# A decoder step on one core: the order of the instructions comes from another timing model of the scheduler

## The chip, the core and the metric

The kernel runs on one core of a Trainium2 chip. The core has five engines that run at the same time: PE (TensorE, matrix products), DVE (VectorE), ACT (ScalarE), POOL (GpSimd) and SP (SyncE, which here only issues transfers). Each engine runs its own instructions strictly in the order in which the program holds them; between engines there are only semaphores. An instruction that waits therefore holds up all that stands behind it on its engine, ready or not. The metric is the device time of one execution in microseconds (us).

## The reference

One inference step of a trunk of four layers over 256 prompt tokens and 8 x 4 sample tokens, model width 1024, MLP width 4096, float32. Each layer has a token mixer and an MLP; the mixers are SGU, RG-LRU, S5 and again SGU.

```python
for layer in range(DEPTH):
    h = rmsnorm(x, p['norm_mix'][layer])
    out = chunk_sgu(h, ...) | rglru_block(h, ...) | s5_block(h, ...)   # by layer % 3
    x = x + out
    x = x + sqrelu_ffn(rmsnorm(x, p['norm_ffn'][layer]), p['w_ff1'][layer], p['w_ff2'][layer])
return rmsnorm(x, p['norm_f']), ...

def rmsnorm(x, g):
    return x * lax.rsqrt(jnp.mean(x * x, axis=-1, keepdims=True) + EPS) * g
def sqrelu_ffn(h, w1, w2):
    return jnp.square(jax.nn.relu(h @ w1)) @ w2
```

RG-LRU is a projection, a causal convolution of width 4, two gates (block-diagonal products and sigmoids), a linear recurrence in time, and a product with a gelu branch before `w_out`. S5 is a complex diagonal state-space layer whose matrices follow from few parameters.

## The kernel before, in words

All activations stay on chip, features on the partitions: eight tiles `x[k]` of [128, 288 tokens]. A float32 product is made of three passes in a rounded float32 format over operands split in two: `whi*xh`, `whi*xl`, `wlo*xh` (`mm3`, lines 273 to 275). The weights are 176 chunks of 1 MiB, used one after the other. SP loads chunk after chunk (`raw`, line 179), ACT rounds it to `whi` (line 202), DVE forms the rest `wlo` (line 203), in two pieces each; there are three buffers for each of the three. Most chunks are used by 48 matmuls of 288 columns. The chunks are numbered through the layers: 0 to 11 first SGU, 12 to 43 its MLP (FFN0), 44 to 55 RG-LRU, 56 to 87 its MLP (FFN1), and so on.

A norm is applied late. `norm_tile` splits the unscaled `x` into `xh` (ACT, line 284) and `xl` (DVE, line 285); `norm_square` squares each tile (ACT, line 296, two buffers `sq`) and POOL adds the squares up in `ss` (line 297). PE sums `ss` over the features with one product with ones (line 311, tile `acc<-ss,ones`), DVE makes the factor from it (lines 315, 316), and in the MLP that factor is needed only after the second product (line 411). In the MLP, ACT takes the relu (line 388), DVE squares it (394), ACT and DVE split it into `hh` and `hl` (269, 270), and the second product uses these. The first and the second half of the MLP's width come one after the other.

The tables of the S5 layer are formed beside FFN0 and FFN1, in 49 pieces that `spare()` records between the other work. For each of eight tiles `m` of S5: `s5_inputs` (POOL) loads `bt` (line 827) and `qb` (line 830) with transfers that POOL itself issues, forms `bi` by products (836 to 838, each twice) and stores it (840); `s5_powers` and `s5_kernels` (DVE) load `cc`, `bs`, form `cn` and `bq`, PE multiplies them (line 881), POOL clears `kt` (line 884), ACT copies into it (887); `s5_table` (POOL, 897 to 906) forms `tab`. `qb`, `bt` and `bi` have two buffers, `kt` one.

The RG-LRU mixer forms its eight x tiles first (chunks 44 to 47, `evac_x`: lines 605 to 609 give the convolved `xc`), then the gates of each pair of tiles: products on PE (line 623, `sec<-xc,wab`), tanh and exp on ACT (624 to 628), the algebra on POOL and DVE (635 to 641), square root (647), the scan on DVE (660); chunks 48 to 51 form the gelu branch, POOL multiplies the two (682, 683) and splits the result into `gyh` (ACT) and `gyl` (POOL, 685), and chunks 52 to 55 are W_out.

The order in which an engine's instructions stand is not the order of the code. The library's tile scheduler orders the recorded instructions, by priorities (the place in the code; `spare()` lowers the priority of its pieces by 300 places), by dependences and buffers, and by the times at which a timing model says that an engine is free and an operand is ready:

```python
def spare(upto=0):
    if len(background) > (upto or 0):
        with tc.high_priority(offset=-PRI_SPARE):
            background.pop(0)(state['bg'])
```

## Time and profile before

| | us |
|---|---|
| median of three runs | 1320.63 (1314.42 to 1326.06) |
| span of the profiled execution | 1312.3 |
| PE, DVE, ACT, POOL busy in it | 1266.0, 926.8, 617.9, 376.4 |

The profile is one execution. A row of a timeline gives the start (us from the start of the span), the duration, the engine, the line, the operation, output and inputs with their shape, how many in a row there are, and in brackets the idle time of the engine before it and what ended it. A row of windows gives for a stretch the busy time of each engine and in brackets how many of its instructions started in it, then the clock granted to PE (1 is 2.4 GHz), the share of the transfer engines that is busy and what they moved.

### The profile page before, as it was taken

The numbers are of one execution on the slowest core, as the hardware profiler recorded it, in microseconds if no ns is written. First come the engines' busy times: TensorE is split into PE (matmuls) and PEld (weight loads), VectorE is DVE, ScalarE is ACT, GpSimd is POOL, SyncE is SP. The second block draws the span as 40 slices with busy tenths as digits, with TensorE's granted clock in tenths as the row PEclk, the third lists the DMA queues.
The fourth block names the chain that finished last, engine by engine and source line by source line (L and its number), as shares of the span: only waits on it lengthen the run. The fifth ranks groups of instructions, "written<-read, shape, count | busy, mean of one in ns | idle before, by whom it ended". The sixth has DMA issues, their size and how long they took to land.

```text
span 1312.3 us, 23910 instructions
## 1 busy us (share of the span) xinstructions
PE 1266.0 (96%) x9802; PEld 1223.4 (93%) x9802; DVE 926.8 (71%) x1437; ACT 617.9 (47%) x1019; POOL 376.4 (29%) x524
## 2 busy tenths in 40 slices
PE   8999999799979998999999999999999999999997
PEld 7999999699968997998999899999999999999997
DVE  8899759686787897748768756655666677655653
ACT  5745532354564644236443345534544645534541
POOL 2237647501258485860121200000012221000010
PEclk9999999899988998999999999999999999999998
DMA  8526666555431767546567434554446334544431
GB/s 290 207 97 205 225 185 220 181 197 194 145 121 62 232 214 243 185 153 217 182 241 257 159 131 159 177 176 162 161 161 217 135 133 160 190 161 160 161 129 37
DMA packets 47006, 230.33 MB, mean 176 GB/s; under 512 B 7904, under 2 KB 13712, under 8 KB 24368
## 3 DMA queue, kind: packets, MB, share of 16 engines
q1 hardware_dynamic: 38016, 209.63, 46.5%
q0 software_dynamic: 8016, 18.45, 4.4%
q8 instruction: 77, 1.26, 0.4%
q10 hardware_dynamic: 864, 0.72, 0.2%
q14 instruction: 33, 0.27, 0.1%
HBM read 214.17 MB, written 14.60 MB: 174 GB/s over the span
## 4 chain that ended last, share of the span: by engine, by line
PE 63%; POOL 14%; DMA 9%; DVE 8%; issue 2%; ACT 2%; SPq 0%; DVEq 0%; POOLq 0%; ACTq 0%
PE acc L275 19%; PE acc L273 19%; PE acc L274 19%; DMA qb<-qd 6%; DMA scr<-tab 3%; POOL tab L905 2%; DVE wlo L203 2%; POOL ta L903 2%; POOL tab L904 2%; POOL bi L836 2%; POOL tb L903 1%; POOL bt L837 1%; POOL bi L838 1%; PE sec L959 1%; PE sec L881 1%
## 5 line engine op out<-in xcount | busy, mean ns | idle before, releaser
L202 ACT ACTIVATE whi<-raw 128x1024 fp32r<-128x1024 f32 (+1 forms) x354 | 363.6, 1048 | 330.9 <-PE acc L274 267.0
L203 DVE TENSOR_TENSOR wlo<-raw,whi 128x1024 fp32r<-128x1024 f32 (+1 forms) x354 | 443.4, 1269 | 106.4 <-ACT whi L202 104.6
L273 PE MATMUL acc<-xh,whi 128*128 128x288 f32 x1472 | 442.3, 301 | 8.0 <-ACT whi L202 7.1
L275 PE MATMUL acc<-xh,wlo 128*128 128x288 f32 x1472 | 440.1, 300 | 7.1 <-DVE wlo L203 7.0
L274 PE MATMUL acc<-xl,whi 128*128 128x288 f32 x1472 | 434.4, 295 | 2.1 <-DVE xl L285 2.1
L273 PE MATMUL acc<-hh,whi 128*128 128x288 f32 x1024 | 305.5, 298 | 3.9 <-ACT hh L269 3.9
L274 PE MATMUL acc<-hl,whi 128*128 128x288 f32 x1024 | 304.7, 298 | 1.1 <-DVE hl L270 1.1
L275 PE MATMUL acc<-hh,wlo 128*128 128x288 f32 x1024 | 303.2, 296 | 0.0
L273 PEld LDWEIGHTS acc<-xh,whi 128*128 128x128 f32 x1472 | 278.6, 189 | 12.5 <-ACT whi L202 8.1
L275 PEld LDWEIGHTS acc<-xh,wlo 128*128 128x128 f32 x1472 | 277.7, 189 | 11.8 <-DVE wlo L203 10.1
L274 PEld LDWEIGHTS acc<-xl,whi 128*128 128x128 f32 x1472 | 282.2, 192 | 5.9 <-DVE xl L285 3.4
L297 POOL TENSOR_TENSOR ss<-ss,sq 128x288 f32<-128x288 f32 x62 | 67.7, 1092 | 566.5 <-ACT sq L296 566.0
L273 PEld LDWEIGHTS acc<-hh,whi 128*128 128x128 f32 x1024 | 192.6, 188 | 7.3 <-ACT hh L269 4.7
L274 PEld LDWEIGHTS acc<-hl,whi 128*128 128x128 f32 x1024 | 192.9, 188 | 4.5 <-issue 2.6
L275 PEld LDWEIGHTS acc<-hh,wlo 128*128 128x128 f32 x1024 | 193.6, 189 | 2.4 <-issue 2.2
L411 DVE TENSOR_TENSOR t<-acc,r 128x288 f32<-128x288 f32 x64 | 29.1, 455 | 138.8 <-PE acc L275 138.8
L269 ACT ACTIVATE hh<-t 128x288 fp32r<-128x288 f32 x128 | 56.9, 444 | 125.6 <-DVE t L394 125.6
L270 DVE TENSOR_TENSOR hl<-t,hh 128x288 fp32r<-128x288 f32 x128 | 63.3, 495 | 25.8 <-ACT hh L269 24.4
L394 DVE TENSOR_TENSOR t<-t 128x288 f32<-128x288 f32 x128 | 64.8, 506 | 4.7 <-ACT t L388 4.7
L388 ACT ACTIVATE t<-acc 128x288 f32<-128x288 f32 x128 | 51.0, 398 | 21.8 <-PE acc L275 18.1
L285 DVE SCALAR_TENSOR_TENSOR xl<-x,aux,xh 128x288 fp32r<-128x288 f32 x64 | 52.9, 834 | 7.3 <-ACT xh L284 7.3
L284 ACT ACTIVATE xh<-x,aux 128x288 fp32r<-128x288 f32 x64 | 33.5, 527 | 33.9 <-DVE x L519 15.5
(324 smaller groups left out, 1508.1 us busy)
## 6 DMA issues: line engine op xcount, KB each, us to landing
raw<-in_wall SPq DMA_DIRECT2D x173, 1024.0 KB, 4.8
sci<-scr SPq DMA_DIRECT2D x8, 768.0 KB, 6.3
sco<-scr SPq DMA_DIRECT2D x8, 768.0 KB, 5.6
bt<-in_bt POOLq DMA_DIRECT2D x8, 512.0 KB, 7.7
scr<-cn SPq DMA_DIRECT2D x8, 512.0 KB, 5.0
qb<-qd POOLq DMA_DIRECT2D x8, 512.0 KB, 13.4
scr<-bi POOLq DMA_DIRECT2D x8, 512.0 KB, 6.1
raw<-in_wall SPq DMA_DIRECT2D x4, 512.0 KB, 8.9
```

The source lines that it names most:

```text
L202: nc.scalar.activation(h[:, c], self.raw[i][:, c], AF.Copy)
L203: nc.vector.tensor_tensor(l[:, c], self.raw[i][:, c], h[:, c].bitcast(F32), op=OP.subtract)
L269: S.activation(h, src, AF.Copy)
L270: V.tensor_tensor(l, src, h.bitcast(F32), op=OP.subtract)
L273: PE.matmul(ps, wh, h, start=first, stop=False)
L274: PE.matmul(ps, wh, l, start=False, stop=False)
L275: PE.matmul(ps, wl, h, start=False, stop=last)
L285: V.scalar_tensor_tensor(xl[k], x[k], A[g][:, k:k + 1], xh[k].bitcast(F32), op0=OP.mult, op1=OP.subtract)
L297: G.tensor_tensor(state['ss'], state['ss'], q, op=OP.add)
L388: i = S.activation(q, ps[:, :T], AF.Relu)
L394: V.tensor_tensor(q2, q, q, op=OP.mult)
L903: eng.tensor_tensor(t[:, :, :, :w], tab[:, :, :, :w], fb, op=OP.mult)
```

## The change

The scheduler's context is opened with another argument. The library then orders the recorded instructions with its more detailed timing simulator in place of its default one. The rest of the diff removes comments.

```diff
-    with tile.TileContext(nc) as tc:
+    with tile.TileContext(nc, schedule_with_timeline_sim=True) as tc:
         body(tc, a, o, layers)
```

The instructions are the same, apart from two more loads of an activation table on ACT in the RG-LRU gates. Their order changes on all engines. Three places follow. In the rows, the number behind a name tells one tile from the next of its kind.

The first is POOL in the second half of FFN0, where it forms `bi` of the S5 tiles 2 (`bi_2613`) and 3 (`bi_3094`). Before:

```order
L827 DMA bt_3090<-in_bt 128x2x512
L840 DMA scr_115<-bi_2168 128x1024
L836 TENSOR_TENSOR bi_2613<-bt_2609,qb_2611 128x512
L837 TENSOR_TENSOR bt_218_2614<-bt_2609,qb_2611 128x512
L836 TENSOR_TENSOR bi_2613<-bt_2609,qb_2611 128x512
L838 TENSOR_TENSOR bi_2613<-bi_2613,bt_218_2614 128x512
L830 DMA qb_3092<-qd 128x1x1024
L837 TENSOR_TENSOR bt_226_2745<-bt_2609,qb_2611 128x512
L838 TENSOR_TENSOR bi_2613<-bi_2613,bt_226_2745 128x512
L840 DMA scr_116<-bi_2613 128x1024
L836 TENSOR_TENSOR bi_3094<-bt_3090,qb_3092 128x512
```

After:

```order
L827 DMA bt_3090<-in_bt 128x2x512
L830 DMA qb_3092<-qd 128x1x1024
L840 DMA scr_115<-bi_2168 128x1024
L837 TENSOR_TENSOR bt_218_2614<-bt_2609,qb_2611 128x512
L836 TENSOR_TENSOR bi_2613<-bt_2609,qb_2611 128x512 x2
L838 TENSOR_TENSOR bi_2613<-bi_2613,bt_218_2614 128x512
L836 TENSOR_TENSOR bi_3094<-bt_3090,qb_3092 128x512 x2
```

The load of `qb` for tile 3 (L830) moved up past the store L840 and four products, and the first two products that need it moved up too. The memset of `kt` (L884) stays behind all products of tile 3.

The second is POOL at the start of FFN1, where the last squares of the norm are added (`ss_4957`) and `bi` of the S5 tile 4 (`bi_5164`) begins. Before:

```order
L297 TENSOR_TENSOR ss_4957<-ss_4957,sq_5020 128x288
L897 COPY tab_5472<-s5rc 128x4
L898 COPY tab_5472<-s5rs 128x4
L884 MEMSET kt_5591 128x512
L297 TENSOR_TENSOR ss_4957<-ss_4957,sq_5032 128x288
L903 TENSOR_TENSOR ta_5473<-tab_5472,s5rc 128x8
L903 TENSOR_TENSOR tb_5474<-tab_5472,s5rs 128x8
L827 DMA bt_5669<-in_bt 128x2x512
L297 TENSOR_TENSOR ss_4957<-ss_4957,sq_5044 128x288
L836 TENSOR_TENSOR bi_5164<-bt_5160,qb_5162 128x512
```

After, with the first product of `bi_5164` directly ahead of these rows:

```order
L837 TENSOR_TENSOR bt_435_5165<-bt_5160,qb_5162 128x512
L836 TENSOR_TENSOR bi_5164<-bt_5160,qb_5162 128x512
L297 TENSOR_TENSOR ss_4957<-ss_4957,sq_5020 128x288
L904 TENSOR_TENSOR tab_5472<-ta_5473,tb_5474 128x4
L905 TENSOR_TENSOR tab_5472<-ta_5473,tb_5474 128x4
L838 TENSOR_TENSOR bi_5164<-bi_5164,bt_435_5165 128x512
L297 TENSOR_TENSOR ss_4957<-ss_4957,sq_5032 128x288
L903 TENSOR_TENSOR ta_5473<-tab_5472,s5rc 128x8x2
L903 TENSOR_TENSOR tb_5474<-tab_5472,s5rs 128x8x2
L836 TENSOR_TENSOR bi_5673<-bt_5669,qb_5671 128x512 x2
L837 TENSOR_TENSOR bt_454_5322<-bt_5160,qb_5162 128x512
L297 TENSOR_TENSOR ss_4957<-ss_4957,sq_5044 128x288
```

The last three of the seven adds (L297) stood ahead of the first `bi` and stand behind it now; the last of them also stands behind two products of the next tile (`bi_5673`). The load of `qb_5162` stands behind two adds, where it stood behind four. On PE the norm's product L311 still follows directly on chunk 57 and stands ahead of all of chunk 58, except that the eight products L881 of S5 tile 4 now stand between chunk 57 and L311.

The third is PE in the RG-LRU mixer at the gate products of the last pair (`xc_4385`). Before, in chunk 49, first column tile (`acc_4523`):

```order
L273 MATMUL acc_4523<-xh_92,whi_4392 128x288
L623 MATMUL sec_4470<-xc_4385,wab 128x312
L623 MATMUL sec_4471<-xc_4385,wab 128x312
L623 MATMUL sec_4478<-xc_4385,wab 128x312
L274 MATMUL acc_4523<-xl_100,whi_4392 128x288
```

After, in chunk 50, second column tile (`acc_4607`):

```order
L274 MATMUL acc_4607<-xl_101,whi_4460 128x288
L623 MATMUL sec_4470<-xc_4385,wab 128x312
L623 MATMUL sec_4471<-xc_4385,wab 128x312
L623 MATMUL sec_4478<-xc_4385,wab 128x312
L275 MATMUL acc_4607<-xh_93,wlo_4461 128x288
```

The gate products moved behind some 72 matmuls of the chunks 49 and 50.

## Rows read from the trace of the kernel before

**Rows 1.** The page: busy time of each engine, and the chain that ended last.

```profile
PE 1266.0 (96%) x9802; PEld 1223.4 (93%) x9802; DVE 926.8 (71%) x1437; ACT 617.9 (47%) x1019; POOL 376.4 (29%) x524
PE 63%; POOL 14%; DMA 9%; DVE 8%; issue 2%; ACT 2%; SPq 0%; DVEq 0%; POOLq 0%; ACTq 0%
```

**Rows 2.** Windows: stretch, us, busy of PE, PEld, DVE, ACT, POOL; clock, transfers.

```profile
820.00:853.00 33.00, 33.00 (x252) 33.00 (x251) 20.55 (x32) 18.29 (x31) 0.00 (x0) 1.00 0.51 175
351.00:421.00 70.00, 59.28 (x365) 54.65 (x365) 58.90 (x87) 45.43 (x75) 44.02 (x64) 0.88 0.26 91
400.35:428.88 28.53, 25.83 (x172) 25.25 (x171) 20.33 (x23) 12.59 (x21) 25.28 (x35) 0.88 0.27 93
460.38:473.85 13.47, 13.11 (x99) 12.87 (x99) 13.38 (x10) 4.39 (x8) 13.45 (x14) 1.00 0.44 147
459.00:492.00 33.00, 32.27 (x242) 31.80 (x241) 31.25 (x36) 13.95 (x25) 28.88 (x30) 1.00 0.63 212
492.00:525.00 33.00, 27.98 (x186) 26.41 (x185) 23.57 (x29) 15.12 (x22) 16.97 (x21) 0.90 0.75 243
```

**Rows 3.** Timeline of ACT and PE, second half of FFN0.

```profile
253.27 1.11 ACT L887 ACTIVATE kt<-sec 32x128 f32<-32x128 f32 x4 [11.87 <-POOL kt L884]
...
255.81 0.61 PE L273 MATMUL acc<-xh,whi 128*128 128x288 f32 x1 [6.63 <-ACT whi L202]
...
258.20 0.44 PE L273 MATMUL acc<-xh,whi 128*128 128x288 f32 x1
258.44 0.44 PE L274 MATMUL acc<-xl,whi 128*128 128x288 f32 x1
```

**Rows 4.** Timeline of PE, RG-LRU: gate products, start and end of W_out.

```profile
385.79 3.46 PE L623 MATMUL sec<-xc,wab 128*128 128x312 f32 x6 [6.24 <-DVE xc L609]
...
412.10 0.47 PE L273 MATMUL acc<-gyh,whi 128*128 128x288 f32 x1 [2.15 <-ACT whi L202]
...
440.87 0.29 PE L273 MATMUL acc<-xh,whi 128*128 128x288 f32 x1
```

**Rows 5.** Timeline of PE and ACT, FFN1.

```profile
454.96 0.65 PE L311 MATMUL acc<-ss,ones 128*128 128x288 f32 x2
...
506.77 0.61 PE L273 MATMUL acc<-hh,whi 128*128 128x288 f32 x1 [1.88 <-ACT hh L269]
...
527.79 0.41 PE L881 MATMUL sec<-cn,bq 128*32 128x128 f32 x2
...
532.78 0.40 PE L274 MATMUL acc<-hl,whi 128*128 128x288 f32 x1
...
586.41 1.11 ACT L887 ACTIVATE kt<-sec 32x128 f32<-32x128 f32 x4 [12.49 <-POOL kt L884]
...
589.91 0.40 PE L275 MATMUL acc<-xh,wlo 128*128 128x288 f32 x1 [0.73 <-DVE wlo L203]
```

**Rows 6.** Timeline of POOL, second half of FFN0.

```profile
222.94 0.56 POOL L840 DMA_DIRECT2D scr<-bi  x1
...
234.08 0.74 POOL L830 DMA_DIRECT2D qb<-qd  x1
...
244.09 1.29 POOL L836 TENSOR_TENSOR bi<-bt,qb 128x512 f32<-128x512 f32 x1 [5.58 <-DMA qb<-qd]
...
252.69 0.55 POOL L884 MEMSET kt<- 128x512 f32 x1
```

**Rows 7.** Timeline of POOL, start of FFN1.

```profile
441.65 0.76 POOL L827 DMA_DIRECT2D bt<-in_bt  x1
...
443.19 0.72 POOL L830 DMA_DIRECT2D qb<-qd  x1
...
448.75 1.44 POOL L297 TENSOR_TENSOR ss<-ss,sq 128x288 f32<-128x288 f32 x1
460.38 1.29 POOL L836 TENSOR_TENSOR bi<-bt,qb 128x512 f32<-128x512 f32 x1 [10.18 <-DMA qb<-qd]
```

**Rows 8.** Line 830, all eight transfers into qb, us from issue to landing.

```profile
DMA to landing us min/median/max: 9.8/13.4/17.4
```

## The prediction, made before the changed kernel was run

> **What bounds the kernel now.** I read the page's busy shares first. TensorE (PE) is busy 96% of the span, VectorE (DVE) 71%, ScalarE (ACT) 47%, GpSimd (POOL) 29%, and the chain that ended last is 63% PE [rows 1]. So the kernel is bound by the matmuls, and a new order can win only what PE stands idle. How much is that? In an undisturbed stretch PE starts 252 matmuls in 33 us, one per 0.131 us [rows 2]. The second view is PE's timeline, read for rows with idle time in front. The large ones are few: 6.63 us in the first MLP (FFN0) [rows 3], 6.24 and 2.15 us in the RG-LRU mixer [rows 4], 1.88 us and several neighbours where FFN1's second product starts [rows 5], 0.73 us near 590 [rows 5]. The third view is POOL's timeline, because the idle engine is usually waiting for a queue, and the queues run strictly in the order the scheduler wrote. There the reader sees POOL waiting for the transfer into `qb` (5.58 us in FFN0, 10.18 us in FFN1 [rows 6, 7]). An in-order queue that waits for a transfer delays everything behind it; what stands behind it is what the change decides.
>
> **The change, part by part.** No work is added except two activation-table loads in the RG-LRU gates; every term is a row that stands elsewhere.
>
> FFN0. The `qb` load is issued right behind the `bt` load, where `scr` is issued now (222.94 us), and not at 234.08 [rows 6]. Today the chain is: `qb` lands, `bi` starts at 244.09, six products of this tile follow, the memset of `kt` comes at 252.69, ACT's copy L887 starts at 253.27 after 11.87 us of waiting, the split of the next weights stands behind it, and PE runs dry for 6.63 us [rows 3, 6]. Issue to landing of `qb` is 9.8, 13.4 or 17.4 us (least, median, most) [rows 8]. From 222.9 the median gives 236.3; POOL reaches `bi` of this tile at about 234 in either case. From there the remaining rows, 12.2 us by today's durations, put the memset at 248.5 where it is now at 252.7: 4.2 us earlier (0.7 to 6.2 by the ends of the landing time). PE's wait shrinks by that much, to about 2.4 us. Behind the long wait 19 matmuls start 0.24 us apart instead of 0.13 [rows 3], that is the 1.2 GHz level, 2.1 us; a short wait should not bring them. With 0.41 us of follow-on wait the gain is **7** (1 to 9).
>
> RG-LRU. The gate products L623 of the last pair move from chunk 49 to chunk 50, some 72 matmuls later, so PE has 9.6 us of other work before it needs `xc`; the others move likewise. The waits of 6.24 and 2.15 us should go, and with them a stretch at the lower clock. But what comes next is not PE. DVE is busy 58.9 of the 70 us from 351 to 421, and POOL 25.3 of the 28.5 us in which it forms the gated outputs [rows 2]. The first of these can't start before the first pair's scan on DVE, in front of which the new order puts no less work than now, so it stays near 400 to 402, and the last output near 428 (now 428.9). Only the end is shorter: W_out's last chunk is 48 matmuls, 6.3 us, so W_out ends near 435; now the next product starts at 440.87 [rows 4]. I take **5** (0 to 9), not the 10 that the PE waits alone would give.
>
> FFN1, its start, the one part that loses. PE forms the norm's sum with matmul L311 in the middle of the first product, now at 454.96 [rows 5]. It needs eight squares added up by POOL; the last add is at 448.75, before `bi` starts to wait for `qb` [rows 7]. In the new order three of the adds stand behind `bi`. `qb` is issued behind two adds and not four, near 441.5. It lands at 451.3, 454.9 or 458.9 by the three landing times; this very transfer took 17.2 us (443.19 to 460.38 [rows 7]), so I take 456.8, between the median and that. Behind it 14 POOL rows end with the last add: 1.29+1.50+1.29 for `bi`, 0.82 add, 0.42+1.19 table, 1.50 `bi`, 1.03 add, 1.43 table, 2.58 for the next tile's `bi`, 1.31, 1.44 add, in all 15.8; the nearest stretch, 14 rows of these kinds in a row, has 13.45 [rows 2]. So L311 comes at 472.6, 17.6 later than now. Nothing of the next chunk stands in front of it on PE, only the S5 product L881, which leaves its place at 527.79, where it and eight neighbours take 5.0 us instead of 1.0 [rows 5]: 4.0 back. A lower clock after the wait as in FFN0: 2.1. The loss is **15.7**. The lower end is set by POOL's own rows even if `qb` came at once: two adds end near 440.7, then by today's durations 0.76 and 0.72 for the two DMA issues, 1.39 table copies, two adds, 0.51 memset, 1.5 for the next two issues, 0.6 products and the wait for ACT's later squares bring POOL to `bi` near 449, and 15.8 more to 464.8; the loss is 6 to 8. The upper end is 17.4 us and a clock penalty twice as long, 20.
>
> A rule bears on this term. The Trainium skill ("DMA: Bandwidth & Descriptors", Anatomy of one DMA, SWDGE path) gives a transfer issued by POOL as about 2 us plus its bytes over 436 GB/s; for these 512 KB that makes an estimate of 3.2 us. By that the term would be some 8 us smaller and the whole 8 us faster; this trace disagrees, its fastest of eight is 9.8 us [rows 8].
>
> While PE waits, ACT stands at a square whose buffer POOL frees late, and DVE at L315 behind L311. DVE has S5 rows pulled forward to fill most of that time, so I cost it at nothing; if it idles, the price is in the rivals.
>
> FFN1, second product. In 492 to 525 PE starts 186 matmuls instead of 252: 8.6 us short, since DVE was full before it (31.25 of 33 us) [rows 2]. The S5 rows done during the wait take load from DVE there: **3** (0 to 7). Near 590, ACT waits 12.49 us for the memset of `kt`, which now stands about 110 POOL rows earlier; PE's 0.73 us and its neighbours are worth **2** (1 to 2.5) [rows 5].
>
> Start-up and the first mixer (S5 parameters pulled forward beside a full DVE) and the S5 layer move a little both ways: 0, plus or minus 3.
>
> Sum: -7 -5 -3 -2 +15.7 = -1.3, so a profiled span of 1311 against 1312.3. That execution is 8.3 us under the median of 1320.6, so the median becomes about **1319**.
>
> **Rivals.** *The hold-up is small and the gains full.* `qb` lands in 9.8 us, POOL's rows take 13.5, no lower clock: L311 at 464.8, loss 464.8 - 455.0 - 4.0 = 5.8; gains 9+9+6+2 = 26. Sum -20: 1300. For it: the transfer has fewer competitors when issued early. Against: raw weights move in the same stretch, and the same load has just taken 17.2 us.
> *DVE is held as long as PE and becomes the bound.* Place: DVE's row L315, behind which the splits of the next weights and FFN1's second operands wait. DVE needs 31.25 of 33 us in 459 to 492 [rows 2], so what it idles there is not caught up. If it stands 16 us before L315 and the pulled-forward rows cover only 2 of them, PE loses some 14 more where its second product starts, and the 3 of that term go too: sum +16, 1336. It decides once DVE's uncovered idle time passes some 11 us. For it: DVE's saturation. Against: the rows `bq`, `cn` and two splits stand in front of L315.
> *POOL's own rows decide, not the transfer:* L311 at 464.8, 4.0 given back, a lower clock of 2.1 and the gains as I take them, sum -17+7.9 = -9: 1311. The eight landing times speak against it [rows 8]. The page of the Trainium skill named above speaks for it.
> *Nothing moves:* all waits only change place, 1320.
>
> **How the numbers follow.** My sum 0.35 (its own range 1310 to 1328), full gains 0.30 (1300), DVE held 0.23 (1336), POOL's rows 0.07, nothing 0.05. A measurement here tells about 1%, 13 us, from no change. Faster by over 1% is the second case and a little of the fourth: 0.31; slower the third: 0.23; within 1% the rest: 0.46. The range runs to the two outer cases: 1299 to 1338.
>
> **What would show it.** After: PE's row before L311 in FFN1 has an idle time of 10 to 18 us with a POOL add (`ss`) as its releaser, and POOL's `bi` in front of it waits for `qb`. FFN0's wait is under 3 us and the matmuls behind it are 0.13 apart. The rows L623 have no wait over 1 us, yet W_out ends only some 5 us earlier against its own start of the mixer. I am wrong if L311 has no wait (then `qb` landed early), if the RG-LRU gives 10, or if the waits return in a place that I cost at nothing.

## The result, and the profile after

| | before | after |
|---|---|---|
| median of the runs taken together, us | 1323.14 (1314.42 to 1326.06) | 1338.20 (1335.40 to 1342.24) |
| after to before | | 1.0134, interval 1.0094 to 1.0175 |
| span of the profiled execution, us | 1312.3 | 1334.0 |

The change makes the kernel 1.3% slower, more than the 1% that tells a change from none here. The forecast was 1319, its range ended at 1338, and the median came out 0.2 us above that end.

The busy times of the engines in the profile after, and the chain that ended last, against [rows 1]:

```profile
PE 1261.7 (95%) x9802; PEld 1225.7 (92%) x9802; DVE 927.0 (69%) x1437; ACT 618.0 (46%) x1021; POOL 379.4 (28%) x524
PE 72%; DVE 9%; POOL 8%; DMA 6%; issue 3%; ACT 2%; SPq 0%; DVEq 0%; POOLq 0%; ACTq 0%
```

The engines do the same work in sum, and PE's busy time even fell by 4.3 us: the 21.7 us of the span, and these 4.3, are idle time of PE. Its large waits stand in three places, in the timeline of PE after (start, duration, engine, line, tiles, count, and in brackets the idle time before and its releaser); the second row is one of the gate products:

```profile
262.92 0.61 PE L273 MATMUL acc<-xh,whi 128*128 128x288 f32 x1 [12.66 <-ACT t L388]
...
394.55 1.81 PE L623 MATMUL sec<-xc,wab 128*128 128x312 f32 x6 [1.53 <-ACT whi L202]
...
417.26 0.85 PE L273 MATMUL acc<-gyh,whi 128*128 128x288 f32 x2 [11.91 <-ACT gyh L684]
...
421.39 0.61 PE L274 MATMUL acc<-gyl,whi 128*128 128x288 f32 x1 [2.56 <-POOL gyl L685]
...
482.19 1.33 PE L311 MATMUL acc<-ss,ones 128*128 128x288 f32 x2 [18.74 <-POOL ss L297]
```

The wait in FFN0 has grown from 6.63 to 12.66 us [rows 3]. The gate products L623 no longer wait for `xc` [rows 4]; one wait of 1.53 us for ACT is left among them. But W_out has a wait of 11.91 and one of 2.56 us where there was 2.15. L311 waits 18.74 us for POOL's adds.

Two timelines of POOL after, FFN0 and the start of FFN1:

```profile
207.00 1.29 POOL L836 TENSOR_TENSOR bi<-bt,qb 128x512 f32<-128x512 f32 x1 [21.37 <-DMA qb<-qd]
...
222.16 0.70 POOL L830 DMA_DIRECT2D qb<-qd  x1
...
231.63 0.72 POOL L830 DMA_DIRECT2D qb<-qd  x1
...
239.61 1.28 POOL L837 TENSOR_TENSOR bt<-bt,qb 128x512 f32<-128x512 f32 x1 [6.71 <-DMA qb<-qd]
...
258.72 0.54 POOL L884 MEMSET kt<- 128x512 f32 x1
...
465.14 1.26 POOL L836 TENSOR_TENSOR bi<-bt,qb 128x512 f32<-128x512 f32 x1 [7.94 <-DMA qb<-qd]
...
480.37 1.77 POOL L297 TENSOR_TENSOR ss<-ss,sq 128x288 f32<-128x288 f32 x1
```

In FFN0 the memset of `kt` comes at 258.72 instead of 252.69 [rows 6]. In FFN1 `bi` starts 4.8 us later than before [rows 7], and the last add, which stood at 448.75, ends at 482.1.

**Where the time went.** The time of a place in the program is the start of the matmul (L273 to L275) that opens a chunk, 48 matmuls to the chunk. The table gives that start after, less the same start before; a step between two lines is what the stretch lost. Such a difference of starts is called a lag below. The second column anticipates experiment e8, a second profile of the unchanged kernel (span 1313.1): it is the fairer base, since the two profiles of before differ by some 5 us in the second half of FFN0 alone. Lags named with an experiment are against the first profile unless the text says otherwise.

| opens chunk | what lies ahead of it | after less first profile of before, us | after less second, us |
|---|---|---|---|
| 28 | start-up, first SGU, half of FFN0 | +2.5 | +2.9 |
| 46 | rest of FFN0 | +5.6 | +0.8 |
| 50 | gate products | -8.1 | -12.6 |
| 56 | W_out | +8.1 | +3.6 |
| 58 | L311 | +27.7 | +23.2 |
| 64 | rest of FFN1's first product | +29.9 | +26.7 |
| 66 | first two chunks of the second product | +27.5 | +24.0 |
| 68 | place where L881 stood | +23.2 | +19.8 |
| 78 | place near 588 | +20.6 | +17.4 |
| last | S5 and the rest | +22.0 | +20.3 |

The large step is the start of FFN1, 19.6 us. The gate products won 13.4 us and W_out gave back 16.2.

### The profile page after: what moved, and what is told of

Read it like the earlier page. It is cut to its first block, busy times and chain, and to the rows that moved or that the text cites. A ratio compares the mean times of both kernels' runs of the same rounds, so it can differ in the third digit from the quotient of the medians.

```text
span 1334.0 us, 24021 instructions
## 1 busy us (share of the span) xinstructions
PE 1261.7 (95%) x9802; PEld 1225.7 (92%) x9802; DVE 927.0 (69%) x1437; ACT 618.0 (46%) x1021; POOL 379.4 (28%) x524
## 4 chain that ended last, share of the span: by engine, by line
PE 72%; DVE 9%; POOL 8%; DMA 6%; issue 3%; ACT 2%; SPq 0%; DVEq 0%; POOLq 0%; ACTq 0%
PE acc L273 22%; PE acc L275 22%; PE acc L274 22%; DVE wlo L203 3%; DMA qb<-qd 2%; DMA bs<-in_bs 1%; POOL tb L903 1%; DMA scr<-bi 1%; POOL ta L903 1%; DVE t L394 1%; PE sec L881 1%; PE sec L959 1%; PE acc L997 1%; DMA scr<-tab 1%; POOL tab L904 1%
## 5 line engine op out<-in xcount | busy, mean ns | idle before, releaser
L202 ACT ACTIVATE whi<-raw 128x1024 fp32r<-128x1024 f32 (+1 forms) x354 | 353.5, 1046 | 341.4 <-PE acc L274 278.2
L273 PE MATMUL acc<-xh,whi 128*128 128x288 f32 x1472 | 439.2, 301 | 14.7 <-ACT t L388 13.4
L275 PE MATMUL acc<-xh,wlo 128*128 128x288 f32 x1472 | 439.6, 300 | 3.1 <-DVE wlo L203 3.1
L273 PE MATMUL acc<-hh,whi 128*128 128x288 f32 x1024 | 304.1, 298 | 2.7 <-ACT hh L269 2.7
L275 PE MATMUL acc<-hh,wlo 128*128 128x288 f32 x1024 | 303.2, 296 | 0.0
L273 PEld LDWEIGHTS acc<-xh,whi 128*128 128x128 f32 x1472 | 278.1, 190 | 19.2 <-ACT t L388 13.8
L275 PEld LDWEIGHTS acc<-xh,wlo 128*128 128x128 f32 x1472 | 278.4, 189 | 6.2 <-DVE wlo L203 4.4
L297 POOL TENSOR_TENSOR ss<-ss,sq 128x288 f32<-128x288 f32 x62 | 67.3, 1086 | 559.1 <-ACT sq L296 558.8
L273 PEld LDWEIGHTS acc<-hh,whi 128*128 128x128 f32 x1024 | 192.5, 188 | 5.2 <-ACT hh L269 3.3
L275 PEld LDWEIGHTS acc<-hh,wlo 128*128 128x128 f32 x1024 | 194.0, 189 | 2.0 <-issue 2.0
L269 ACT ACTIVATE hh<-t 128x288 fp32r<-128x288 f32 x128 | 56.0, 444 | 94.6 <-DVE t L394 92.3
L394 DVE TENSOR_TENSOR t<-t 128x288 f32<-128x288 f32 x128 | 69.5, 555 | 10.3 <-ACT t L388 9.6
L270 DVE TENSOR_TENSOR hl<-t,hh 128x288 fp32r<-128x288 f32 x128 | 63.2, 507 | 9.3 <-ACT hh L269 5.6
L285 DVE SCALAR_TENSOR_TENSOR xl<-x,aux,xh 128x288 fp32r<-128x288 f32 x64 | 48.8, 768 | 6.8 <-ACT xh L284 6.8
```

The costliest lines, as they stand in the source:

```text
L202: nc.scalar.activation(h[:, c], self.raw[i][:, c], AF.Copy)
L269: S.activation(h, src, AF.Copy)
L270: V.tensor_tensor(l, src, h.bitcast(F32), op=OP.subtract)
L273: PE.matmul(ps, wh, h, start=first, stop=False)
L275: PE.matmul(ps, wl, h, start=False, stop=last)
L285: V.scalar_tensor_tensor(xl[k], x[k], A[g][:, k:k + 1], xh[k].bitcast(F32), op0=OP.mult, op1=OP.subtract)
```

## Experiments

Each ratio is to the kernel before, run on the same chip in the same group. The order on an engine is called unchanged where every row stands as in the kernel compared with.

### FFN1: is it the wait before L311, or what POOL does beside DVE?

**e1**, the changed kernel with the adds in front of `bi`:

```diff
+        with tc.issue_after(state['ss_last']) if m >= 4 else nullcontext():
+            eng.tensor_tensor(bi[:, n], bt[:, 0], qb[:, :, n], op=OP.mult)
...
```

(The two rows behind it likewise; `ss_last` is the last L297.) The scheduler then also moved rows of PE (L881 among them), DVE, ACT and SP between 460 and 566 us, so not the adds alone differ.

> The changed kernel, with one thing undone: POOL's products for bi of the S5 tiles 4 to 7 are queued behind the last add of the norm's squares in FFN1. Theory 1 (the loss at the start of FFN1 is PE's wait at L311 for adds that stand behind bi): the wait of 18.9 us before L311 falls to under 3 us, the stages before it stay as they are, and the time falls by 14 to 18 us, to a ratio against the kernel before of about 1.001 (0.998 to 1.004). Rival (the wait is handed on: DVE and ACT are late anyway in FFN1): the wait before L311 goes, but PE's idle time comes back within the next 60 us and the time falls by less than 6 us, ratio over 1.008.

Measured: 1330.20 us (1328.43 to 1332.93), ratio 1.0077 (1.0048 to 1.0106), span 1328.5. The wait before L311 is gone and the lag at chunk 58 falls from 27.7 to 12.9 us, but it is 21.9 at chunk 64 and 23.4 at chunk 66: PE waits for DVE in the rest of the first product (6.81 us for `wlo` at 508.51) and, for less, in the second. The windows of e1 (stretch, busy of PE, PEld, DVE, ACT, POOL with the number of rows, clock, transfers), and the mean duration of DVE's row L270 between 485 and 515:

```profile
492.00:525.00 33.00, 23.46 (x149) 22.53 (x148) 32.34 (x22) 9.02 (x17) 30.82 (x37) 0.84 0.50 175
```

```profile
L270 DVE TENSOR_TENSOR hl<-t,hh 128x288 fp32r<-128x288 f32 x9 | 17.3, 1940 | 0.1
```

DVE is busy 32.34 of 33 us and gets only 22 rows started. In 820 to 853 of the kernel before, where POOL has no row at all [rows 2], the same row lasts 454 ns:

```profile
L270 DVE TENSOR_TENSOR hl<-t,hh 128x288 fp32r<-128x288 f32 x11 | 5.0, 454 | 2.6 <-ACT hh L269 2.6
```

One row of e1 shows the difference. From the timeline of DVE and POOL:

```profile
497.87 7.23 DVE L270 TENSOR_TENSOR hl<-t,hh 128x288 fp32r<-128x288 f32 x1
...
498.98 1.31 POOL L837 TENSOR_TENSOR bt<-bt,qb 128x512 f32<-128x512 f32 x1
500.24 2.51 POOL L836 TENSOR_TENSOR bi<-bt,qb 128x512 f32<-128x512 f32 x2
...
503.53 1.25 POOL L838 TENSOR_TENSOR bi<-bi,bt 128x512 f32<-128x512 f32 x1
504.73 0.60 POOL L906 DMA_DIRECT2D scr<-tab  x1
```

The row L270 lasts 7.23 us and ends at 505.10, 0.3 us behind a series of six tensor rows that POOL runs without a break from 498.98 to 504.78. (A transfer issue of 0.60 us, at 498.37 on POOL, stood inside it as well and did not end it, so how the two engines take turns is not shown.) Most of what the wait before L311 had cost is here paid to DVE. The gain is 8 us by the medians, between the two expectations and nearer to the rival's.

**e7**, e1 with POOL's rows thinned: of the three rows of each `bi` product of tiles 4 to 7 the second product and the difference are left out, so that `bi` of these tiles is not the reference's:

```diff
-            eng.tensor_tensor(t1, bt[:, 1], qb[:, :, 1 - n], op=OP.mult)
-            eng.tensor_tensor(bi[:, n], bi[:, n], t1, op=(OP.subtract, OP.add)[n])
+            if m < 4:
+                eng.tensor_tensor(t1, bt[:, 1], qb[:, :, 1 - n], op=OP.mult)
+                eng.tensor_tensor(bi[:, n], bi[:, n], t1, op=(OP.subtract, OP.add)[n])
```

> e1 (the changed kernel with the adds in front) and, for S5 tiles 4 to 7, two of the three POOL rows of each bi product left out (the second product and the difference, so bi of these tiles and the output that depends on it are not the reference's); all orders on PE, DVE, ACT and SP are those of e1. It takes some 20 us of POOL's rows out of 440 to 560. Theory (DVE's rows are stretched while POOL runs its own tensor rows, and that made DVE the bound of 492 to 525): hl, t and wlo return to 0.45, 0.45 and 1.2 us each for most of the stretch, PE's waits of 6.97 and 3.12 us shrink by over half, and the lag at chunk 66 against before falls from +23 to +12 or less. Rival (DVE is full by its own rows, POOL is no matter): lag at chunk 66 stays at +20 or more, DVE still busy 32 of 33 us.

Measured: 1313.05 us (1310.52 to 1316.69), ratio 0.9962 (0.9938 to 0.9985), span 1309.9. The lag at chunk 66 is 4.5 us instead of 23.4. The same window and the same row in e7:

```profile
492.00:525.00 33.00, 33.00 (x251) 33.00 (x250) 26.47 (x30) 15.12 (x23) 21.45 (x31) 1.00 0.79 257
```

```profile
L270 DVE TENSOR_TENSOR hl<-t,hh 128x288 fp32r<-128x288 f32 x12 | 5.8, 500 | 0.8 <-ACT hh L269 0.5
```

PE starts 251 matmuls where it started 149, and L270 takes 500 ns instead of 1940. No order but POOL's was touched, and the transfers moved more than in e1 (257 against 175 GB/s), so they are not the cause: it is POOL's rows that stretch DVE's. The Trainium skill ("SBUF — State Buffer", Who interferes with whom, and Summary: rules for kernel authors) has the rule: a DVE instruction with two SBUF inputs contends with a POOL instruction that reads SBUF, and the second to issue waits until the first is done. The trace agrees on who is slowed (L270 reads two tiles in SBUF), but not on for how long: 7.23 us is several times POOL's longest row there.

**e9**, the changed kernel thinned in the same way, its adds left where the change has them, so that four kernels make a square:

> The changed kernel with its own places for the adds of the squares, and for S5 tiles 4 to 7 two of the three POOL rows of each bi product left out as in e7 (bi of these tiles and what depends on it are not the reference's). With after, e1 and e7 it makes a square: adds pinned or not, POOL's rows full or thinned. Theory H (the wait before L311 is lost for good by a kernel bound by PE, except for what before loses later in the second product, 8.6 us, and near 588, 2.6 us): L311 waits 10 to 16 us, the lag at chunk 58 is +20 to +25, at chunk 66 +12 to +17, at the end +9 to +14; ratio to before 1.006 to 1.010. Theory C (POOL's rows beside DVE are nearly the whole loss of FFN1): the wait before L311 is there, but by the end the lag is 0 to +4, as in e7 (-2.0); ratio 0.997 to 1.002.

Measured: 1320.67 us (1319.97 to 1322.51), ratio 1.0027 (1.0011 to 1.0042), span 1318.9. L311 still waits:

```profile
475.59 1.33 PE L311 MATMUL acc<-ss,ones 128*128 128x288 f32 x2 [11.31 <-POOL ss L297]
```

The lag is 21.1 us at chunk 58, 13.4 at chunk 66 and 6.9 at the end. That lies between the two expectations: theory H had 9 to 14 at the end, theory C 0 to 4. The square is not quite clean, since the scheduler moved some fourteen rows of DVE and two of ACT between 462 and 504 us as well.

**e13**, the kernel before thinned in the same way; the orders of PE, DVE, ACT and SP are unchanged:

> The kernel before with two of the three POOL rows of each bi product of S5 tiles 4 to 7 left out (bi of these tiles and what depends on it are not the reference's); the orders of PE, DVE, ACT and SP are those of before, word for word. In the changed kernel the same thinning was worth 15.1 us (after against e9) and 18.9 us (e1 against e7). Theory (the order of before keeps POOL's rows off DVE better, so that the change made the loss): at most the 8.6 us that PE misses in the second product and the 2.6 near 588 can come back: 4 to 10 us at the end against the profile of before, ratio 0.992 to 0.997. Rival (POOL's rows cost either order the same, and the change only added the wait before L311): 14 us or more, ratio 0.989 or less.

Measured: 1306.74 us (1303.90 to 1310.80), ratio 0.9898 (0.9854 to 0.9942), span 1303.4. Against e8, from which it differs by at most 0.2 us from chunk 34 to chunk 64, it wins 7.2 us by chunk 66 and 9.7 by the last matmul. Its window, and below it the same stretch of e8:

```profile
492.00:525.00 33.00, 31.75 (x235) 30.83 (x233) 23.20 (x26) 12.95 (x19) 15.52 (x19) 1.00 0.76 248
```

```profile
492.00:525.00 33.00, 27.84 (x184) 26.59 (x183) 23.20 (x27) 13.86 (x21) 18.72 (x20) 0.90 0.73 216
```

The square, with the old order beside it (end: start of the last matmul, less that of e8):

| | POOL's rows full | thinned | thinning |
|---|---|---|---|
| changed, adds behind `bi` | 1.0134, +20.3 us | 1.0027, +5.2 | 1.1%, 15.1 us |
| changed, adds in front (e1, e7) | 1.0077, +15.3 | 0.9962, -3.7 | 1.2%, 18.9 |
| before | 1, 0 | 0.9898, -9.7 | 1.0%, 9.7 |

Read down: the adds behind `bi`, with their wait before L311, cost 0.6 to 0.7% (5.1 and 8.9 us in the profiles). Only the thinned pair shows it clear of the intervals; those of the changed kernel and e1 overlap. Read across: the thinned rows of POOL cost about twice that, by what they stretch on DVE and by what stands behind them on POOL together. Their price is there in the old order too. Whether the new order raises it stays open: the profiles say so (15 to 19 us against 9.7), the ratios do not (1.1 and 1.2% against 1.0%, whose interval is 0.6 to 1.5%).

### FFN0: was the wait made by the new order?

**e2**, the changed kernel with `kt` cleared by DVE in place of POOL, and **e3**, the kernel before with the same edit:

```diff
-        G.memset(kt, 0.0)
+        V.memset(kt, 0.0)
```

> The changed kernel, with the clearing of kt (L884) on DVE instead of POOL. Theory 2 (PE's wait of 12.8 us in FFN0 is ACT standing at its copy into kt because POOL clears it only behind the bi chain): ACT's wait of 24 us before L887 there goes, PE's wait falls under 2 us, and with the matmuls at the lower clock behind it the time falls by 11 to 16 us, ratio about 1.003. Rival (the split of the weights is late by itself, or DVE is as late as POOL): PE still waits over 6 us in FFN0 and the time falls by less than 5 us, ratio over 1.009.

> The kernel before, with the clearing of kt (L884) on DVE instead of POOL; no other engine's order changes. Theory 2: PE's wait of 6.6 us near 250 and those near 588 go, with the slow matmuls behind the first, 8 to 12 us less, ratio 0.991 to 0.994. Rival: DVE, busy 31.9 of 33 us just before that place, clears kt as late as POOL did; under 3 us, ratio over 0.998.

Measured: e2 1320.10 us (1314.22 to 1323.26), ratio 0.9995 (0.9971 to 1.0020), span 1321.5; e3 1312.51 us (1309.55 to 1316.15), ratio 0.9939 (0.9916 to 0.9961), span 1307.9. In both the large wait of FFN0 is gone (in e2 4.0 us for `wlo` remain), so the memset was the link between POOL's queue and PE in either order. In e2 the median fell by 18 us, more than the 11 to 16 expected, the profile by 12; the scheduler reordered FFN1 too, where 13.58 us before L311 and a new 13.04 us before L881 stand in the timeline. In e3 POOL's order changes at FFN1 as well, against its expectation: the adds fall behind `bi`, and the old scheduler makes the same mistake as the new one:

```profile
452.51 1.33 PE L311 MATMUL acc<-ss,ones 128*128 128x288 f32 x2 [8.61 <-POOL ss L297]
```

Of 11.6 us won by the end of FFN0, e3 keeps 3.6 at the end.

**e8**, the kernel before once more, nothing edited:

> The kernel before, unchanged, for a second profile: its profiled span was 8.8 us under the median of its runs, and the first pair of qb transfers landed after 15.6 and 16.5 us there, while the five other profiles (one of them with the same order up to that point) show 19.9 to 25.6. Theory (the landing of this pair differs by execution, and the short one was a lucky one): it lands after 20 to 25 us here, POOL's first bi starts at 205 to 207 instead of 200.9, PE's wait in FFN0 is 10 to 13 us instead of 6.6, and the span is 1317 to 1321. Rival (the order decides): landing 15 to 17 us, PE's wait 6 to 7, span 1311 to 1314.

Measured: 1315.16 us, span 1313.1. From its timelines of PE and of POOL:

```profile
261.20 0.61 PE L273 MATMUL acc<-xh,whi 128*128 128x288 f32 x1 [13.79 <-ACT whi L202]
```

```profile
201.30 3.77 POOL L836 TENSOR_TENSOR bi<-bt,qb 128x512 f32<-128x512 f32 x1 [20.07 <-DMA qb<-qd]
...
258.08 0.55 POOL L884 MEMSET kt<- 128x512 f32 x1
```

The unchanged kernel waits 13.79 us in FFN0 here, more than the changed one. The first two `qb` transfers landed after 21.3 and 26.0 us, where the first profile had 15.6 and 16.5. In the fifteen profiles of this study the pair's first transfer took 15.6 to 22.7 us, and 19.9 or more in ten of them. e13, whose POOL stands in the old order there too, had a short pair (16.3 us) but a long load for tile 2 (17.5 us, 10.9 in the first profile), and PE waited 13.15 us. So the 6.63 us of [rows 3] was a short sample, and the new order did not make the wait. The span did not follow as far as expected: this execution won 3.1 us back elsewhere.

**e12**, the changed kernel with one thing undone, the place of the `qb` load that the prediction priced:

```diff
-            G.dma_start(qb.rearrange('p q n c -> p (q n c)'),
+            with tc.issue_after(s5['last']) if m == 3 else nullcontext():
+                G.dma_start(qb.rearrange('p q n c -> p (q n c)'),
...
```

(`s5['last']` is the last row of the first half of the tile before.)

> The changed kernel with one thing undone: the load of qb for S5 tile 3 stands on POOL behind the products of tile 2's first half again, as it does before; all other orders are those of the changed kernel. The four profiles with the changed order there show PE waits of 12.8, 13.9, 14.8 and 15.1 us in FFN0. Theory (the earlier issue is worth the 4 to 7 us that the prediction gave it, and something further up ate them): undoing it costs as much, kt's memset comes at 263 to 266 and PE waits 17 to 20 us. Rival (an earlier issue wins nothing, since the load then shares the transfer engines with tile 2's loads and the store and lands no sooner): PE's wait stays at 12 to 15 us.

Measured: 1337.40 us, span 1335.6. Up to 222 us its POOL runs within 0.3 us of the changed kernel. PE's row:

```profile
264.86 0.61 PE L273 MATMUL acc<-xh,whi 128*128 128x288 f32 x1 [14.49 <-ACT t L388]
```

The wait is 14.49 us, as the rival said, and the row starts 1.9 us later than in the changed kernel, not 4 to 7. Tile 3's load, issued 11 us later, lands only 6.8 us later (at 252.0 and not 245.2), since it takes 9.3 us and not 13.5. The fifteen profiles agree: that load takes 13.5 to 20.5 us in the six in which it is issued 8.5 to 9.5 us behind tile 2's, and 9.1 to 11.6 in eight of the nine others (15.8 in e5). The rest of the difference is that tile 2's load took 13.9 us here and 17.3 there. Whether the load behind it makes it slower, which is the rival's reason, is not shown: in the nine profiles with no load behind it, it took 10.9 to 19.1 us, in the six others 14.7 to 18.0. One execution can't settle the price of the early issue.

### RG-LRU: why W_out gave back what the gates won

**e4**, the changed kernel with the exponential of the gates written into four buffers in place of one:

```diff
-                st['gr'], st['gi'], st['t2'], st['e'] = f_('gr', 4), f_('gi', 4), f_('t2g', 4), f_('eg')
+                st['gr'], st['gi'], st['t2'], st['e'] = f_('gr', 4), f_('gi', 4), f_('t2g', 4), f_('av', 4)
...
-                rc, av = d, f_('av', 4)[:, :, :JW]
+                state['n'] += 1; rc, av = d, ex
```

> The changed kernel, with the exponential of the RG-LRU gates written into the tile that later takes av (four buffers) instead of a tile of its own with one buffer. Theory 3 (W_out starts late because the last pair's exponential waits for L638 of the pair before, and the square roots of all pairs stand behind it on ACT): ACT's wait of 3.8 us before L628 goes, the square roots start 4 to 8 us earlier, PE's waits of 12.1 and 2.9 us at W_out shrink to 5 to 9 in all, the time falls by 5 to 9 us, ratio about 1.008. Rival (DVE's and POOL's rows themselves set the outputs): the square roots come earlier, the first product of outputs does not, the time falls by less than 3 us, ratio over 1.011.

Measured: 1336.40 us (1335.61 to 1340.29), ratio 1.0124 (1.0077 to 1.0171), span 1338.5.

```profile
417.73 0.85 PE L273 MATMUL acc<-gyh,whi 128*128 128x288 f32 x2 [10.21 <-ACT gyh L684]
```

The wait at W_out is 10.21 us and a second one of 3.74 follows, 13.95 in all against 14.47: no gain, as the rival said. ACT's stall before L628 is gone, but the roots' table load comes only 1.2 us earlier, counted from chunk 46. The single buffer was not what set the outputs.

What sets them is in the timelines of ACT, DVE and POOL after, beside which the answering rows of e8 stand in the second fence:

```profile
402.88 1.28 ACT L647 ACT_TABLE_LOAD   x1
404.17 1.96 ACT L647 ACTIVATE t2g<-t2g 128x624 f32<-128x624 f32 x3
406.04 1.99 ACT L202 ACTIVATE whi<-raw 128x1024 fp32r<-128x1024 f32 x2
408.04 1.28 ACT L625 ACT_TABLE_LOAD   x1
...
409.87 1.28 ACT L647 ACT_TABLE_LOAD   x1
...
413.20 1.78 ACT L680 ACTIVATE gg<-gg 128x288 f32<-128x288 f32 x5
...
404.93 1.69 DVE L651 SCALAR_TENSOR_TENSOR t2g<-gr,t2g 128x624 f32<-128x624 f32 x1 [3.83 <-ACT t2g L647]
...
413.73 1.67 POOL L682 TENSOR_TENSOR t<-gg,t2g 128x256 f32<-128x256 f32 x1 [0.68 <-DVE t2g L660]
```

```profile
397.24 1.28 ACT L647 ACT_TABLE_LOAD   x1
...
402.40 1.12 ACT L680 ACTIVATE gg<-gg 128x288 f32<-128x288 f32 x3
...
405.08 1.06 POOL L682 TENSOR_TENSOR t<-gg,t2g 128x256 f32<-128x256 f32 x1
```

All square roots are queued behind the last exponential, in the code itself:

```python
def root(p):
    t2 = st['pairs'][p][3]
    with tc.issue_after(st['exp'].ins):
        st['sqrt'] = S.activation(t2, t2, AF.Sqrt)
```

So the scan of the first pair needs a root that stands behind the gates of the last pair, and DVE's first row behind the roots waits for ACT (3.83 us at 404.93). Moving the last pair's products back on PE moves the first output back. The new order adds something on ACT: the two pieces of a chunk's `whi` and two more table loads stand between the first root and the first gelu L680, the other operand of the first output, which comes 9.0 us behind the root and not 3.9 as in e8.

**e6 and e10** test this on a better kernel, e5 (below), by giving the four products of the last pair a lower priority (96 and 150 places), which puts them 44 and 87 to 90 matmuls later; in the trace after, the change has put them 76 (the first) to 91 (the last) later, where the order fences ahead say some 72:

```diff
-                    for n in range(2):
-                        PE.matmul(pg[n][:, :JW], wab[:, n, m], xc, start=True, stop=True)
+                    with tc.high_priority(offset=-96 if p in (3,) else 0):
+                        [PE.matmul(pg[n][:, :JW], wab[:, n, m], xc, start=True, stop=True) for n in range(2)]
```

> e5 and, in addition, the four gate products L623 of the last RG-LRU pair 44 matmuls later on PE (5.8 us of other work in front of them, about as long as the 6.24 us that PE waited for xc). Theory (PE had other work, and the products start at the same time as before, so the roots L647 and the gated outputs do not move): the wait of 6.2 us goes and W_out starts 5 us earlier than its operands, so part of it returns as a wait for gyh: 2 to 5 us better than e5, 1303 to 1306 us. Rival (the outputs are the bound in any case): the 6.2 us come back in full before W_out's second and third chunk: e5's time within 1 us.

> e6 with the four gate products L623 of the last RG-LRU pair 87 matmuls later than before (11.4 us) instead of 44 (5.8 us); the change moved them by about 74. Theory (the roots L647 wait for the last pair's exponentials, so what the products are moved past the time at which xc is ready, 385.8 in before, comes back at W_out): no wait at L623, but the roots start some 5 us later than in e6, PE waits some 5 us more for gyh before W_out (3.3 + 1.8 in e6), and the end is 3 to 6 us later than e6: 1309 to 1312. Rival (the outputs are set by DVE's and POOL's own rows, wherever the products stand): W_out's waits and the end as in e6 within 1.5 us.

Measured: e6 1305.98 us (1301.76 to 1309.67), ratio 0.9901 (0.9871 to 0.9932), span 1300.0; e10 1310.19 us (1307.98 to 1310.75), ratio 0.9924 (0.9875 to 0.9973), span 1308.9. From the timelines of ACT and PE, e6 first, e10 second:

```profile
381.63 1.28 ACT L647 ACT_TABLE_LOAD   x1
...
395.01 0.40 PE L273 MATMUL acc<-gyh,whi 128*128 128x288 f32 x1 [3.18 <-ACT gyh L684]
396.90 0.61 PE L274 MATMUL acc<-gyl,whi 128*128 128x288 f32 x1 [1.50 <-POOL gyl L685]
```

```profile
388.86 1.28 ACT L647 ACT_TABLE_LOAD   x1
...
400.73 0.85 PE L273 MATMUL acc<-gyh,whi 128*128 128x288 f32 x2 [7.38 <-ACT gyh L684]
402.63 0.61 PE L274 MATMUL acc<-gyl,whi 128*128 128x288 f32 x1 [0.81 <-POOL gyl L685]
```

Moved by about the length of the wait (44 matmuls, 5.8 us), the products cost nothing: in e5 the roots' table load stands at 381.92. Moved by 87, the load comes 7.2 us later and PE waits 3.5 us more at W_out (some 5 were expected). The medians are as the theory had them, e10 4.2 us behind e6, but by the ratios it is 3 us, inside their intervals; what shows the mechanism is the rows. In the profile e10 ends 8.9 us behind e6; the part beyond W_out was lost in FFN1, in waits for `wlo`, `hh` and `hl`.

e10 also tells how much of the change's loss this is. Its last pair of products stands nearly where the change has it. In the profiles the mixer takes 88.0 us from chunk 46 to chunk 56 in e5, 83.9 in e6 and 88.0 in e10: the late place gives back all that the wait at L623 was worth, and no more. The changed kernel takes 92.3 against 89.4 in e8. So 2.8 us are left for the rest of the new order, in which the first product of W_out starts 60.6 us behind chunk 46, against 57.6 in e10. ACT's rows ahead of the gelu do not explain it alone: in e4 the first gelu comes 3.1 us earlier than in the changed kernel, counted from chunk 46, and the mixer is only 0.4 us shorter, since PE then waits longer for POOL's `gyl`. What makes the 2.8 us stays open.

### Versions that beat both kernels

**e5** is the kernel before with `kt` cleared on DVE (e3) and the adds in front (e1's edit); **e6** adds the later gate products; **e11** is e6 with POOL's pieces of tiles 6 and 7 held back:

```diff
+                    if layer == 1 and half == 0 and m == 2:
+                        s5['mark'] = G.tensor_copy(bg_([P, 1], 'mk'), q[:, 0:1]).ins
...
+    def held(m, f, *args):
+        with tc.issue_after(s5['mark']) if m >= 6 else nullcontext():
+            f(*args)
```

> The kernel before with kt cleared on DVE (as e3) and, in addition, the bi products of S5 tiles 4 to 7 queued on POOL behind the last add of the norm's squares. Against e3 only POOL's order changes there. Theory (the hold-up before L311 that e3 showed, 8.8 us behind the adds, is a loss of its own): the wait before L311 goes, and about 8 of the 11 us that e3 won in FFN0 reach the end: ratio to before 0.990, 1308 us. Rival (as in e1, DVE is the bound of 459 to 525 and hands the wait on): L311 does not wait, but PE waits for wlo and hl in the second product instead: no more than 2 us better than e3, ratio 0.993, 1312 us.

> e6 with POOL's pieces of S5 tiles 6 and 7 queued behind a copy of one column on POOL that needs the third output of FFN1's second product, so that they start near 515 and not at 495. Theory (POOL's rows beside DVE cost PE the waits for hl and hh between 488 and 500, 9.5 us in e6): the two or three rows of those waits that stand beside tile 6's rows shrink, 2 to 4 us better than e6: 1302 to 1304. Rival (the waits stand beside the rows of tiles 4 and 5, which are not moved): as e6 within 1 us, or later where S5 starts, if tile 7's tables come too late.

Measured: e5 1310.48 us (1306.80 to 1312.43), ratio 0.9930 (0.9908 to 0.9952), span 1306.9; e11 1304.99 us (1302.98 to 1307.00), ratio 0.9903 (0.9866 to 0.9940), span 1301.2. In e5 L311 no longer waits and the lag at chunk 58 is -11.5 us, but -2.0 at chunk 66: as in e1 the wait is handed on to DVE, and e5 is only 1 to 2 us better than e3, by ratio and profile, which is inside the intervals. In e11 PE's waits at 493 to 499 stand beside the rows of tiles 4 and 5, and nothing is won over e6, as its rival said. e6 and e11 are 1% faster than the kernel before, with the default scheduler.

## Why the prediction was wrong

The measured terms are against the second profile of before (the steps of the table above):

| term | forecast, us | measured, us |
|---|---|---|
| start-up and first mixer | 0 | +2.9 |
| FFN0 | -7 | -2.1 |
| RG-LRU | -5 | +2.8 |
| FFN1 start, gross | +19.7 | +19.6 |
| rest of FFN1's first product | in the line above | +3.5 |
| second product | -3 | -2.7 |
| L881 leaving 527.79 | -4.0 | -4.2 |
| near 588 | -2 | -2.4 |
| S5 | 0 | +2.9 |
| sum | -1.3 | +20.3 |

**FFN1 start: right in place and size.** `qb` was issued at 450.15 and 454.14, `bi` waited for it, and from 465.14 to 482.14 POOL needed 17.0 us to the end of the last add, where 14 rows had been taken as 15.8. L311 waits 18.74 us, a little over the 10 to 18 given as the sign. The 19.7 held 2.1 us of lower clock behind the wait; there it is seven matmuls 0.24 us apart, 0.8 us. L881 gave back 4.2, and 588 gave 2.4. The loss was called; the gains of FFN0 and the RG-LRU, which were to balance it, did not come.

A premise of the clock part, that a short wait should not bring the slow matmuls, fails in the trace that was read. Behind the wait of 2.15 us at 412.10 [rows 4] and one of 0.55 us right after it, 22 matmuls of the kernel before stand 0.24 us apart. A window of its PE there (stretch, us, busy, clock, transfers):

```profile
414.00:416.00 2.00, 2.00 (x10) 0.50 0.87 242
```

**FFN0: the step that failed is that POOL reaches `bi` at about 234 in either case.** It took the stretch upstream as given. The first of the pair of `qb` loads landed 6 us later than in the one profile that had been read (206.9 and not 200.8), the load in question was issued at 231.63 and not at 222.9, and the wait moved to the load in front of it (6.71 us at 239.61). The second failure is in the price: a landing time was taken as a property of the transfer, though this load takes 13.5 to 20.5 us behind another one in flight and mostly 9.1 to 11.6 without; 11 us of earlier issue bring the landing 6.8 us forward (e12). The range of this step was also misadded: by its own rows the memset comes 0.2 to 6.5 us earlier, not 0.7 to 6.2. And the profile's wait of 6.63 us was taken as typical, though that execution was known to lie 8.3 us under the median; e8 shows 13.79.

**RG-LRU: the step that failed is that the new order puts no less work in front of the first pair's scan, "so it stays near 400 to 402".** "No less" was taken as "the same", and only DVE's queue was looked at. The scan also waits for a root on ACT, which stands behind the last pair's exponential, which stands behind the very products that the change moved. Against e8 the first output came 8.65 us later, 7.9 without the lag of 0.8 at the start of the mixer. The waits at L623 went as forecast, 13.4 us with their clock, and W_out lost 16.2. e6 and e10 show the boundary: a product can be moved past other work as far as its operand is late, and no further. By e10 the late place explains why nothing was won; the 2.8 us lost on top stay open. ACT's two extra table loads, which the prediction named and gave no price, stand in that stretch; no run took them out.

**Second product: the 3 us came where they were forecast (2.7 over chunks 64 and 65), but 3.5 were lost just ahead of it.** The S5 rows of DVE were pulled forward as expected, but POOL's were pulled forward too. Two windows of after; since after is 23 us late here, the second one is no second product, as in [rows 2], but the rest of the first:

```profile
459.00:492.00 33.00, 14.26 (x107) 13.54 (x106) 29.14 (x33) 9.30 (x18) 26.83 (x29) 0.74 0.63 192
492.00:525.00 33.00, 31.45 (x234) 30.75 (x233) 32.57 (x29) 13.75 (x25) 31.26 (x34) 1.00 0.56 197
```

While PE stood, DVE was busy 29.14 of 33 us, and its only wait there is 3.86 us for a load of `bs`. So the rival that DVE would idle in front of L315 did not happen; that its 1336 is close to the result is luck. Busy was not the same as getting on: beside a POOL that is busy 31.26 of 33 us, 29 rows of DVE filled 32.57 us, and PE waited for `t` and `wlo` (0.70, 0.31 and 0.55 us from 516 to 520). The prediction read busy shares and had no term for one engine slowing another. e1 shows what that means for the largest term: its 19 us are real where they stand, but taking the wait away returns only 0.6%, because DVE, slowed by POOL, is right behind it.

**The terms at nothing** were +2.9 us each: PE waits 2.07 us in the first SGU for ACT's `yh` (at 75.59), and 1.28 and 2.19 us in S5 for loads of `sco` (760.50, 768.81). They lie at the edge of the 3 us allowed, and both on the same side. No run separates them further.

## What to carry to other kernels

A wait removed by issuing an instruction later is worth the wait only if nothing that the instruction feeds is queued for all of its siblings at once; follow its result across every in-order queue to the next wait before booking the gain. A profile is one execution: where a term rests on one transfer's landing, read the same row in a second profile before trusting it. When two engines share work in the same stretch, compare the duration of the same row with the other engine idle and busy, since a busy share counts stretched rows as work.

## What was not expected of the hardware

The DVE row L270, with two inputs in SBUF, lasts up to 16 times as long beside POOL's tensor rows (7.23 us against 0.45 in e1), and 3.9 times in the mean of nine rows (1940 against 500 ns in e7). A `qb` load takes far longer than others of its size, from the transfers issued in the profile after (KB each, median us to landing):

```profile
bt<-in_bt POOLq DMA_DIRECT2D x8, 512.0 KB, 6.7
...
qb<-qd POOLq DMA_DIRECT2D x8, 512.0 KB, 16.1
scr<-bi POOLq DMA_DIRECT2D x8, 512.0 KB, 5.2
```

All three are issued by POOL and move 512 KB; `qb` alone reads each row of a small table 32 times over (the zero step in line 830's address pattern), and its pattern alone begins with a dimension of 4 and not of 128. Whether one of these is the cause was not tried. Over all profiles its landing ranged from 7.8 to 29.7 us.
